# A hybrid decoder layer on one core: when ScalarE makes the decays of the state-space scans

## The chip, the core and the metric

The kernel runs on one core of a Trainium2 chip. Its time is the device time of one execution in microseconds (us). Before the change it took 2337.83 us, the median of three runs (2331.14, 2337.83 and 2346.82).

The engines have short names in the profile: PE is TensorE (PEld its weight loads), DVE is VectorE, ACT is ScalarE, POOL is GpSimd and SP is SyncE, which here only issues transfers.

## What is computed

One layer of a decoder for 2048 tokens of width 1024, with 16 learned meta tokens in front. A normalised input goes through one combined projection into two branches: a Mamba-2 state-space branch (SSD, 16 heads of 64 channels in 4 groups, state 128, chunks of 128 tokens) and a gated linear attention (GLA, 4 heads). Both outputs are gated by sigmoids, projected and added, and an output projection, a residual and a last norm follow. The change concerns the SSD branch:

```python
da = (dt * a).reshape(b, nc, chunk, h).transpose(0, 3, 1, 2)
da_cum = jnp.cumsum(da, axis=-1)
seg = da_cum[..., :, None] - da_cum[..., None, :]
decay = jnp.exp(jnp.where(causal, seg, -jnp.inf))
scores = jnp.einsum('bzthn,bzshn->bhzts', cc, bc)
y_diag = jnp.einsum('bhzts,bzsh,bzshp->bzthp', scores * decay, dtc, xc)
...
def step(s, inp):
    st, dec = inp
    return dec[..., None, None] * s + st, s
...
y_off = jnp.einsum('bzthn,bzhpn,bhzt->bzthp', cc, prev, jnp.exp(da_cum))
return (y_diag + y_off).reshape(b, l, h, p), final
```

The "decays" are `decay` of one chunk for the four heads of one group: a tile of 128 x 4 x 128, which is then multiplied by the masked scores.

## The kernel before

**Two phases.** The first phase (about 0 to 1500 us) runs the projections and both branches for four blocks of 512 tokens. The second phase merges the branches and projects the result out. The change is in the first.

**Projections and scans side by side.** For each block the program goes through four SSD groups (`ssd_proj`) and then four GLA heads (`gla_proj`). Each projection is a generator that yields after every piece of some 24 to 48 wide matmuls. After each piece one `step()` runs every scan that has begun, up to its own next `yield`. So the scan of group g is written in between the projection pieces of group g + 1. For a group there are six pieces: two of `proj_tok`, then four of `proj_feat`, one for each of x0, x1, B and C.

**Emptying the banks.** A projection accumulates in PSUM banks called `pj`, of which there are three. A feature piece takes one bank, in block 0 two, because of the meta tokens. ScalarE empties it with a copy into `cin` (L472) and a scaled copy into `acc` (L473); VectorE adds the three other taps of the convolution (L477), ScalarE takes a Tanh (L480), VectorE finishes the SiLU (L481). The gate chain of a block (`gates`) also uses `pj` banks and has an Abs (L435), an Exp (L437) and a Ln (L438) on ScalarE, and scans on VectorE.

**The SSD scan of one group.** `fetch_cb` (L490) issues, from ScalarE's queue, a transfer that spreads the cumulative decay of four heads and 128 tokens to all 128 partitions (tile `cb`, three buffers). The scan's pieces are then:

- the masked scores of all four chunks: four matmuls (L522) and one multiply by the triangle (L524, tile `scm`);
- `before(c)`: three transposes into a `pt` bank (L538), three VectorE multiplies out of it (L541 to L544), a ScalarE copy of B (L547), and the decay: four Relus with a per-partition bias (L550), one Exp (L552), and VectorE's multiply with the masked scores (L553), into a `sq` tile `dm` (five buffers, one of which holds `scm`);
- `after(c)`: four matmuls that read `dm` (L562), more matmuls with the state (L563, L565), the state update on GpSimd and VectorE (L567, L568), VectorE's output chain (L570 to L575), and on ScalarE a Square with an accumulator for the norm (L577);
- at the end the norm (L592), transposes (L597) and the stores.

**The order of work.** PE's and SyncE's instructions keep the order in which they are written. The order on ScalarE, VectorE and GpSimd is chosen at compile time by a scheduler that simulates the program's time; it may put an instruction ahead of others written earlier if its inputs are there. `tc.keep_in_program_order(ins)` adds one edge for the scheduler: `ins` comes behind the instruction that was written just before it on the same engine. It is an order of issue, not a wait for the end of that instruction.

Of the kernel before, what the change touches and what calls it, by code (L numbers as in the profile page):

```python
# [7 lines left out]
F32 = mybir.dt.float32  # L8
# [3 lines left out]
AF = mybir.ActivationFunctionType  # L12
ALU = mybir.AluOpType

P = 128
# [4 lines left out]
NCH = BLK // P  # L20
# [5 lines left out]
NSQ = 5  # L26
# [14 lines left out]
def trunk_kernel(ctx: ExitStack, tc: tile.TileContext, xm, xmt, w_feat, w_tok, w_zm, w_br, w_o,  # L41
                 cf32, cmsk, pvec, fnw, hvec, gw2, out):
    nc = tc.nc
# [5 lines left out]
    def mk(pool, shape, dt, tag, **kw):  # L49
        cnt[0] += 1  # L50
        return pool.tile(shape, dt, tag=tag, name=f"{tag}_{cnt[0]}", **kw)
# [66 lines left out]
    wk = first.enter_context(tc.tile_pool(name="wk", bufs=2))  # L118
# [6 lines left out]
    def bank(pool, tag):  # L125
        return mk(pool, [P, 512], F32, tag)
# [97 lines left out]
    def rstd_of(ssq, n, scale):  # L224
        r = mk(sm, [P, 4], F32, "rstd")
        nc.vector.tensor_scalar(r[:, :n], ssq, scale, EPS, op0=ALU.mult, op1=ALU.add)
        nc.gpsimd.tensor_tensor(r[:, :n], r[:, :n], mhalf[:, :n], op=ALU.pow)
        return r
# [114 lines left out]
    def new_block(b, u):  # L343
        o = Block()
        o.b, o.u = b, u
        o.m0 = META if b == 0 else 0
        o.tt = o.m0 + BLK
        o.segs_all = [(0, o.tt // 2), (o.tt // 2, o.tt // 2)] if b == 0 else [(0, BLK)]
        o.segs_real = [(o.m0, BLK)]
        o.starts = [o.m0 + c * P for c in range(NCH)]  # L350
        o.chunks = ([(0, META)] if o.m0 else []) + [(a, P) for a in o.starts]
        o.ci0 = 1 if o.m0 else 0
        o.nck = len(o.chunks)
        for nm in ("tkd", "tkc", "wde", "ecu", "dec"):
            setattr(o, nm, mk(bpool, [P, 5, NH], F32, nm, bufs=2))
        o.cumd = mk(dpool, [NH, BLK], F32, "cumd")
        o.g_all = mk(bpool, [P, GH, META + BLK], F32, "g_all")
        o.alr = mk(bpool, [P, 5, 48], F32, "alr")
        o.mov = lambda kt, a, n: tuple(t[:, kt, a:a + n] for t in u)
        return o  # L360
# [125 lines left out]
    cbs = {}  # L486

    def fetch_cb(o, g, c):
        cbs[g, c] = cb = mk(wk, [P, 4, P], F32, "cb", bufs=3)
        nc.scalar.dma_start(cb, o.cumd[4 * g:4 * g + 4, c * P:(c + 1) * P].unsqueeze(0).to_broadcast([P, 4, P]))  # L490

    def ssd_scan(o, g, feats, zs):
        m0, ci0 = o.m0, o.ci0
        tkd, tkc, wde, ecu, dec = o.tkd, o.tkc, o.wde, o.ecu, o.dec
        x0, x1, bf, cf = feats
        fetch_cb(o, g, 0)
        yield
        hs = slice(4 * g, 4 * g + 4)

        def hb(t, n):  # L500
            return t.unsqueeze(2).to_broadcast([n, 4, 64])

        if m0:
            ps = bank(pt, "pt")
            for j, f in enumerate((x0, x1, bf)):
                nc.tensor.transpose(ps[:META, j * P:(j + 1) * P], f[:, :META], ident)
            xw = mk(wk, [P, 4, 64], F32, "c1", bufs=NC1)
            nc.vector.tensor_tensor(xw[:META], ps[:META, :256].rearrange("p (a c) -> p a c", c=64),
                                    hb(wde[:META, 0, hs], META), op=ALU.mult)
            btm = mk(wk, [P, P], F32, "bt")  # L510
            nc.scalar.activation(btm[:META], ps[:META, 256:384], AF.Copy)

        def meta_state():
            ps = bank(pc, "pc")
            nc.tensor.matmul(ps[:, :256], btm[:META], xw[:META].rearrange("p a c -> p (a c)"),
                             start=True, stop=True)
            nc.vector.tensor_copy(s_ssd[:, g], ps[:, :256])

        sc = bank(pc, "pc")
        for c in range(NCH):  # L520
            a = m0 + c * P
            nc.tensor.matmul(sc[:, c * P:(c + 1) * P], bf[:, a:a + P], cf[:, a:a + P], start=True, stop=True)  # L522
        scm = mk(wk, [P, NCH, P], F32, "sq", bufs=NSQ)
        nc.vector.tensor_tensor(scm, sc.rearrange("p (c t) -> p c t", t=P),  # L524
                                tri.unsqueeze(1).to_broadcast([P, NCH, P]), op=ALU.mult)
        yt = mk(wk, [P, NCH, 256], F32, "tok4", bufs=NT4)
        ssq = mk(sm, [P, 4], F32, "ssq")
        held = {}

        def before(c):  # L530
            a = m0 + c * P
            ci = ci0 + c
            if c + 1 < NCH:
                fetch_cb(o, g, c + 1)
            cb = cbs.pop((g, c))
            ps = bank(pt, "pt")
            for j, f in enumerate((x0, x1, bf)):
                nc.tensor.transpose(ps[:, j * P:(j + 1) * P], f[:, a:a + P], ident)  # L538
            px = ps[:, :256].rearrange("p (h c) -> p h c", c=64)
            xdt = mk(wk, [P, 4, 64], F32, "c1", bufs=NC1)  # L540
            nc.vector.tensor_tensor(xdt, px, hb(tkd[:, ci, hs], P), op=ALU.mult)  # L541
            xw = mk(wk, [P, 4, 64], F32, "c1", bufs=NC1)
            nc.vector.tensor_tensor(xw, px, hb(wde[:, ci, hs], P), op=ALU.mult)
            nc.vector.tensor_tensor(yt[:, c].rearrange("p (h c) -> p h c", c=64), px,  # L544
                                    hb(d_skip[:, hs], P), op=ALU.mult)
            bt = mk(wk, [P, P], F32, "bt")
            nc.scalar.activation(bt, ps[:, 256:384], AF.Copy)  # L547
            dm = mk(wk, [P, 4, P], F32, "sq", bufs=NSQ)
            for h in range(4):
                nc.scalar.activation(dm[:, h], cb[:, h], AF.Relu, scale=-1.0,  # L550
                                     bias=tkc[:, ci, 4 * g + h:4 * g + h + 1])
            nc.scalar.activation(dm, dm, AF.Exp, scale=-1.0)  # L552
            nc.vector.tensor_tensor(dm, dm, scm[:, c].unsqueeze(1).to_broadcast([P, 4, P]), op=ALU.mult)  # L553
            held[c] = xdt, xw, bt, dm

        def after(c):
            a = m0 + c * P
            ci = ci0 + c
            xdt, xw, bt, dm = held.pop(c)
            py = bank(pc, "pc")  # L560
            for h in range(4):
                nc.tensor.matmul(py[:, h * 64:(h + 1) * 64], dm[:, h], xdt[:, h], start=True, stop=True)  # L562
            nc.tensor.matmul(py[:, 256:512], cf[:, a:a + P], s_ssd[:, g], start=True, stop=True)  # L563
            pst = bank(pc, "pc")
            nc.tensor.matmul(pst[:, :256], bt, xw.rearrange("p a c -> p (a c)"), start=True, stop=True)  # L565
            sv = s_ssd[:, g].rearrange("p (h c) -> p h c", c=64)
            nc.gpsimd.tensor_tensor(sv, sv, hb(dec[:, ci, hs], P), op=ALU.mult)  # L567
            nc.vector.tensor_tensor(s_ssd[:, g], s_ssd[:, g], pst[:, :256], op=ALU.add)  # L568
            yo = mk(wk, [P, 4, 64], F32, "c1", bufs=NC1)
            nc.vector.tensor_tensor(yo, py[:, 256:512].rearrange("p (h c) -> p h c", c=64),  # L570
                                    hb(ecu[:, ci, hs], P), op=ALU.mult)
            yof = yo.rearrange("p a c -> p (a c)")
            nc.vector.tensor_tensor(yof, yof, py[:, 0:256], op=ALU.add)
            nc.vector.tensor_tensor(yof, yof, yt[:, c], op=ALU.add)
            nc.vector.tensor_tensor(yt[:, c], yof, zs[:, c], op=ALU.mult)  # L575
            jk = mk(wk, [P, 256], BF16, "junk", bufs=1)
            nc.scalar.activation(jk, yt[:, c], AF.Square, accum_out=ssq[:, c:c + 1])  # L577

        before(0)
        yield  # L580
        if m0:
            meta_state()
            yield
        for c in range(1, NCH):
            before(c)
            after(c - 1)
            yield
        after(NCH - 1)
        yield
        r = rstd_of(ssq, 4, 1.0 / 1024)  # L590
        for c in range(NCH):
            nc.scalar.activation(yt[:, c], yt[:, c], AF.Identity, scale=r[:, c:c + 1])  # L592
        yield
        for j in range(2):
            ps = bank(pt, "pt")
            for c in range(NCH):
                nc.tensor.transpose(ps[:, c * P:(c + 1) * P], yt[:, c, j * P:(j + 1) * P], ident)  # L597
            yo = mk(wk, [P, BLK], F32, "gg", bufs=4)
            nc.scalar.activation(yo, ps, AF.Identity, scale=hsw[:, 2 * g + j:2 * g + j + 1])
            nc.scalar.dma_start(y_left[0][o.b][2 * g + j], yo)  # L600
# [226 lines left out]
    with tc.manual_schedule(engines={mybir.EngineType.PE, mybir.EngineType.SP}):  # L827
        for b in range(nblk):
            o = new_block(b, next_u[b])
# [343 lines left out]
```

## Time and profile before

| | |
|---|---|
| median of three runs | 2337.83 us |
| the profiled execution | 2339.7 us |
| its span, first to last instruction | 2337.9 us |
| PE busy | 2247.7 us, 96% |
| PEld busy | 1959.0 us, 84% |
| VectorE busy | 1548.3 us, 66% |
| ScalarE busy | 1180.1 us, 50% |
| GpSimd busy | 673.3 us, 29% |
| mean granted clock of TensorE | 0.985 |
| data moved by DMA | 518.05 MB |

A group in the profile is named by line, engine, operation and tiles, with its count and mean time. A row of the timeline gives the start in us, the duration in us, engine, line, operation, output and input tiles, and how many equal instructions are merged; in brackets stands how long the engine was idle before it and what ended that. A row of waits gives the engine, tile and line that waited, the engine and line waited for, the total in us, how often, and the longest. Matmuls overlap in the pipeline, so their durations are longer than the distance between their starts. PE's clock is given as the share of full speed that was granted.

### The profile page before, as it was taken

What the parts mean: (1) busy time and instruction counts of PE and PEld (TensorE: products, weight loads), DVE (VectorE), ACT (ScalarE), POOL (GpSimd) and SP (SyncE); (2) the same over time, 40 slices, a digit from 0 to 9 for tenths busy, and PEclk for the clock granted to TensorE, in tenths of its full rate; (3) what the DMA queues carried; (4) which work ended last, traced back from release to release, by engine and by line L of the source; (5) the groups of instructions that cost most, each with busy time, mean ns of one, the idle gap of its engine ahead of it and who ended that gap; (6) DMA issues with size and microseconds to landing.
All of it is one profiled execution on the core that took longest, in us unless ns stands there. A gap on an engine that the chain in (4) does not pass through costs nothing. (4 is left out here: it accounts for less than half of the span.)

```text
span 2337.9 us, 36478 instructions
## 1 busy us (share of the span) xinstructions
PE 2247.7 (96%) x12641; PEld 1959.0 (84%) x12641; DVE 1548.3 (66%) x2895; ACT 1180.1 (50%) x2758; POOL 673.3 (29%) x681
## 2 busy tenths in 40 slices
PE   7999999999999999999999999889999999999998
PEld 7899988888878989888988898768888778778786
DVE  5676766676675666576567555764578855678866
ACT  5666644465544455544455534454554445554543
POOL 4344433122221122211112100207424254313231
PEclk9999999999999999999999999889999999999999
DMA  8666866767785666786676655357577876777753
GB/s 304 226 203 213 293 227 204 222 191 240 246 274 184 209 222 210 258 260 221 199 226 212 212 161 163 128 180 245 187 244 268 290 231 202 242 267 262 246 171 120
DMA packets 301545, 518.05 MB, mean 222 GB/s; under 512 B 27696, under 2 KB 143664, under 8 KB 301360
## 3 DMA queue, kind: packets, MB, share of 16 engines
q1 hardware_dynamic: 200400, 402.84, 53.4%
q10 hardware_dynamic: 100960, 112.88, 13.9%
q8 instruction: 99, 1.62, 0.3%
q14 instruction: 86, 0.70, 0.1%
HBM read 368.42 MB, written 147.19 MB: 221 GB/s over the span
## 5 line engine op out<-in xcount | busy, mean ns | idle before, releaser
L183 PE MATMUL pj<-u,whl 128*128 128x512 f32 (+1 forms) x1184 | 449.4, 380 | 15.5 <-ACT acc L473 6.0
L185 PE MATMUL pj<-u,whl 128*128 128x512 f32 (+1 forms) x1184 | 433.5, 366 | 1.4 <-POOL whl L164 0.8
L184 PE MATMUL pj<-u,whl 128*128 128x512 f32 (+1 forms) x1184 | 432.8, 366 | 0.0
L183 PE MATMUL pj<-whl,u 128*128 128x256 f32 (+1 forms) x992 | 289.3, 292 | 1.6 <-ACT u L296 1.5
L185 PE MATMUL pj<-whl,u 128*128 128x256 f32 (+1 forms) x992 | 282.6, 285 | 1.5 <-DVE u L298 1.4
L184 PE MATMUL pj<-whl,u 128*128 128x256 f32 (+1 forms) x992 | 282.3, 285 | 0.3 <-POOL whl L164 0.3
L183 PEld LDWEIGHTS pj<-u,whl 128*128 128x128 f32 x1184 | 227.1, 192 | 54.8 <-ACT acc L473 7.0
L183 PE MATMUL psa<-b,a 128*128 128x512 f32 x640 | 249.7, 394 | 15.0 <-ACT sn L931 11.3
L185 PEld LDWEIGHTS pj<-u,whl 128*128 128x128 f32 x1184 | 226.8, 192 | 37.8 <-POOL whl L164 1.9
L184 PEld LDWEIGHTS pj<-u,whl 128*128 128x128 f32 x1184 | 227.4, 192 | 33.4
L185 PE MATMUL psa<-b,a 128*128 128x512 f32 x640 | 250.8, 392 | 1.4 <-DVE a L915 1.4
L184 PE MATMUL psa<-b,a 128*128 128x512 f32 x640 | 250.2, 391 | 0.0
L894 DVE TENSOR_TENSOR b<-br,b 128x512 fp32r<-128x512 f32 x196 | 151.4, 794 | 62.7 <-ACT b L893 59.8
L183 PEld LDWEIGHTS pj<-whl,u 128*128 128x128 f32 x992 | 190.0, 192 | 3.0 <-ACT u L296 1.8
L185 PEld LDWEIGHTS pj<-whl,u 128*128 128x128 f32 x992 | 189.8, 191 | 2.2 <-DVE u L298 2.2
L184 PEld LDWEIGHTS pj<-whl,u 128*128 128x128 f32 x992 | 190.1, 192 | 1.0 <-POOL whl L164 0.6
L164 POOL TENSOR_TENSOR whl<-wr,whl 128x512 fp32r<-128x512 f32 (+1 forms) x100 | 135.7, 1365 | 186.7 <-ACT whl L163 145.6
L80 POOL TENSOR_TENSOR wr<-wr 128x256 f32<-128x256 f32 x80 | 66.0, 825 | 426.7 <-DMA wr<-y 173.7
L905 POOL TENSOR_TENSOR as<-ar,ar 128x512 f32<-128x512 f32 x40 | 56.3, 1407 | 455.6 <-DMA ar<-in_w_br 211.9
L893 ACT ACTIVATE b<-br 128x512 fp32r<-128x512 f32 x196 | 119.0, 627 | 118.7 <-DMA br<-br_t 46.0
L915 DVE TENSOR_TENSOR a<-ar,a 128x512 fp32r<-128x512 f32 x160 | 128.0, 816 | 72.2 <-ACT a L914 71.8
L477 DVE SCALAR_TENSOR_TENSOR acc<-cin,hcw,acc 128x512 f32<-128x512 f32 (+1 forms) x192 | 154.6, 805 | 30.5 <-ACT acc L473 29.3
(271 smaller groups left out, 5058.4 us busy)
## 6 DMA issues: line engine op xcount, KB each, us to landing
whl<-k_s SPq DMA_DIRECT2D x96, 512.0 KB, 4.4
whl<-k_g SPq DMA_DIRECT2D x96, 512.0 KB, 4.2
whl<-k_v SPq DMA_DIRECT2D x48, 512.0 KB, 3.8
whl<-k_z SPq DMA_DIRECT2D x36, 512.0 KB, 3.8
wr<-in_w_feat SPq DMA_DIRECT2D x64, 256.0 KB, 4.4
k_s<-whl SPq DMA_DIRECT2D x32, 512.0 KB, 3.7
cb<-cumd ACTq DMA_DIRECT2D x64, 256.0 KB, 5.8
y<-gg ACTq DMA_DIRECT2D x64, 256.0 KB, 4.5
```

The costliest lines, as they stand in the source:

```text
L80: nc.gpsimd.tensor_tensor(o, x, y, op=ALU.subtract)
L164: nc.gpsimd.tensor_tensor(hl[:, 1], raw, hl[:, 0].bitcast(F32), op=ALU.subtract)
L183: nc.tensor.matmul(ps, sh, mh, start=first, stop=False, **kw)
L184: nc.tensor.matmul(ps, sh, ml, start=False, stop=False, **kw)
L185: nc.tensor.matmul(ps, sl, mh, start=False, stop=last, **kw)
L477: nc.vector.scalar_tensor_tensor(acc, cin[:, k:k + tt], hcw[:, ti, k:k + 1], acc, op0=ALU.mult, op1=ALU.add)
L893: nc.scalar.activation(t[:, 0], raw, AF.Copy)
L894: nc.vector.tensor_tensor(t[:, 1], raw, t[:, 0].bitcast(F32), op=ALU.subtract)
L905: nc.gpsimd.tensor_tensor(s1, a21, a22, op=ALU.add)
L915: nc.vector.tensor_tensor(t[:, 1], src, t[:, 0].bitcast(F32), op=ALU.subtract)
```

## The change

The decay moves out of `before(c)` into a function of its own, `decay(c)`. It is written one piece earlier: `decay(0)` ahead of `before(0)`, `decay(1)` behind it, and in the loop `decay(c + 1)` behind `after(c - 1)`. Each of its four Relus and its Exp is kept in program order on ScalarE. The broadcasts of chunks 0 and 1 are issued in the scan's first piece, and those of chunks 2 and 3 behind `decay(0)` and `decay(1)`. The numbers of buffers do not change.

```diff
         fetch_cb(o, g, 0)
+        fetch_cb(o, g, 1)
         yield
...
-        held = {}
+        held, dms = {}, {}
+
+
+        def decay(c):
+            ci = ci0 + c
+            cb = cbs.pop((g, c))
+            dm = dms[c] = mk(wk, [P, 4, P], F32, "sq", bufs=NSQ)
+            for h in range(4):
+                tc.keep_in_program_order(
+                    nc.scalar.activation(dm[:, h], cb[:, h], AF.Relu, scale=-1.0,
+                                         bias=tkc[:, ci, 4 * g + h:4 * g + h + 1]))
+            tc.keep_in_program_order(nc.scalar.activation(dm, dm, AF.Exp, scale=-1.0))
+            nc.vector.tensor_tensor(dm, dm, scm[:, c].unsqueeze(1).to_broadcast([P, 4, P]), op=ALU.mult)
+            if c + 2 < NCH:
+                fetch_cb(o, g, c + 2)
 
         def before(c):
             a = m0 + c * P
             ci = ci0 + c
-            if c + 1 < NCH:
-                fetch_cb(o, g, c + 1)
-            cb = cbs.pop((g, c))
...
-            dm = mk(wk, [P, 4, P], F32, "sq", bufs=NSQ)
-            for h in range(4):
-                nc.scalar.activation(dm[:, h], cb[:, h], AF.Relu, scale=-1.0,
-                                     bias=tkc[:, ci, 4 * g + h:4 * g + h + 1])
-            nc.scalar.activation(dm, dm, AF.Exp, scale=-1.0)
-            nc.vector.tensor_tensor(dm, dm, scm[:, c].unsqueeze(1).to_broadcast([P, 4, P]), op=ALU.mult)
-            held[c] = xdt, xw, bt, dm
+            held[c] = xdt, xw, bt
 
         def after(c):
...
-            xdt, xw, bt, dm = held.pop(c)
+            xdt, xw, bt = held.pop(c)
+            dm = dms.pop(c)
...
+        decay(0)
         before(0)
+        decay(1)
         yield
...
             before(c)
             after(c - 1)
+            if c + 1 < NCH:
+                decay(c + 1)
             yield
```

## The prediction

> **What bounds the kernel now.** I read the busy shares first, then a table by stage, then who waits for whom, then the order of time around the waits.
>
> ```profile
> PE 2247.7 (96%) x12641; PEld 1959.0 (84%) x12641; DVE 1548.3 (66%) x2895; ACT 1180.1 (50%) x2758; POOL 673.3 (29%) x681
> ```
>
> TensorE (PE) is busy for 2247.7 us of 2337.9, so all its idle time is 90 us. The change touches only the state-space scans, so I cut out their four stretches, one per block of 512 tokens (columns: stretch, its length, PE, PEld, DVE, ACT and POOL busy, granted clock, DMA share, GB/s).
>
> ```profile
> 50.00:300.00 250.00, 236.47 (x1750) 224.14 (x1749) 175.19 (x320) 157.91 (x402) 108.40 (x99) 0.97 0.70 235
> 480.00:660.00 180.00, 177.94 (x1032) 155.55 (x1031) 124.47 (x266) 102.63 (x263) 48.72 (x69) 0.99 0.74 235
> 844.00:1024.00 180.00, 176.82 (x1027) 154.67 (x1026) 124.12 (x267) 102.35 (x260) 47.22 (x69) 0.99 0.73 232
> 1207.00:1380.00 173.00, 172.85 (x1015) 151.83 (x1015) 118.03 (x253) 97.30 (x246) 35.31 (x53) 1.00 0.65 203
> ```
>
> PE idles 13.5 us in block 0 (250 - 236.47), then 2.1, 3.2 and 0.2 us. That is 19 us in all: whatever the decays cost today, no more than this and some lost clock can come back. PE's order is written out by hand and does not change, so a PE wait that goes is won nearly whole, and one that comes is lost nearly whole. The waits of PE, of the first stretch and (last line) of the decays' readers in the whole run:
>
> ```profile
> PE pj L183 <- ACT acc L473: 6.0, 4, 4.2
> PE pj L183 <- ACT g_all L435: 4.4, 2, 3.1
> ...
> PE pc L562 <- DVE sq L553: 1.7, 1, 1.7
> ```
>
> PE waited for a decay itself (L562 reads what L553 wrote) once, 1.7 us. The larger waits are for a PSUM bank of the projections that ScalarE (ACT) had not yet emptied (L473, L435). ScalarE in order of time before the 4.2 us wait, and PE's first matmul after it:
>
> ```profile
> 138.66 1.56 ACT L550 ACTIVATE sq<-cb,tkc 128x128 f32<-128x128 f32 x5
> ...
> 141.29 0.97 ACT L550 ACTIVATE sq<-cb,tkc 128x128 f32<-128x128 f32 x3
> 142.17 0.61 ACT L552 ACTIVATE sq<-sq 128x512 f32<-128x512 f32 x1
> ...
> 143.37 1.13 ACT L552 ACTIVATE sq<-sq 128x512 f32<-128x512 f32 x2
> 145.22 1.28 ACT L550 ACTIVATE sq<-cb,tkc 128x128 f32<-128x128 f32 x4 [0.72 <-DMA cb<-cumd]
> 146.40 0.37 ACT L472 ACTIVATE cin<-pj 128x264 f32<-128x264 f32 x1
> ...
> 147.28 0.59 PE L183 MATMUL pj<-u,whl 128*128 128x264 f32 x1 [4.19 <-ACT acc L473]
> ```
>
> This is the finding that matters. Nothing holds the decays back today, so the scheduler has put all four chunks of the group at the front of ScalarE's order: 16 Relus (in four rows of 5, 4, 3 and 4; the second is left out) and three of the four Exps run from 138.66 to 146.40, the last four Relus behind a broadcast that had not landed (0.72). Only then come the copies (L472, and L473 behind it) that free PE's bank.
>
> **What the change does, part by part.** No instruction is added or removed: 256 Relus, 64 Exps, 64 multiplies, 64 broadcasts as before. It changes when they come.
>
> *The burst becomes shorter.* At a group's first working piece only chunks 0 and 1 are written; chunk 2 comes one piece on, chunk 3 another. By the rows above a decay is four Relus, 1.28 us, and an Exp, 0.57 (1.13 for two), so 1.8 us, and two are 3.7. In the 4.19 us wait the copy L472 could then start near 143.1 (138.66, two decays, and the 0.7 us of other work that lay between the first Exp and the next two), not at 146.40: 3.3 us won. The other waits on L473, 6.0 - 4.2 = 1.8 us, were partly of this kind: I take 0.7 (bounds 0 and 1.8). The 3.1 us wait for L435 began the same way:
>
> ```profile
> 78.70 1.55 ACT L550 ACTIVATE sq<-cb,tkc 128x128 f32<-128x128 f32 x5
> ...
> 82.88 0.46 ACT L435 ACTIVATE g_all<-pj,pv 128x264 f32<-128x264 f32 x1
> ```
>
> Here 12 Relus and an Exp stood ahead, 4.2 us. Two decays of 1.8 us would stand ahead at worst (0.5 won), one at best (2.4 won); I take 1.5. Together 5.5 us, bounds 3.8 and 7.5.
>
> *Clock lost behind those waits.* The granted clock is column eight here.
>
> ```profile
> 84.00:88.00 4.00, 4.00 (x23) 4.00 (x22) 1.27 (x2) 4.00 (x10) 0.00 (x0) 0.57 0.98 319
> ...
> 147.00:151.00 4.00, 3.72 (x17) 3.72 (x18) 2.93 (x3) 3.15 (x7) 1.48 (x2) 0.50 1.05 372
> ```
>
> In the 4 us after the first wait 0.43 of the clock was missing (1.7 us), after the second 0.50 (2.0 us). I count the second, whose wait nearly goes, and not the first, which is only shortened: 2.0 us, bounds 0 and 3.7.
>
> [...]
>
> *Chunk 0's decay.* Its Exp now follows its own four Relus and need not stand behind those of chunks 1 and 2 (eight Relus, 2.5 us). Today chunk 0 is just in time:
>
> ```profile
> 576.03 0.69 DVE L553 TENSOR_TENSOR sq<-sq,sq 128x512 f32<-128x512 f32 x1 [3.06 <-ACT sq L552]
> ...
> 577.24 0.45 PE L562 MATMUL pc<-c,sq 128*128 128x64 f32 x3
> ...
> 584.82 0.45 PE L562 MATMUL pc<-c,sq 128*128 128x64 f32 x3
> ```
>
> It ends 0.5 us before its reader (the third row is chunk 1's, one piece or 7.6 us on). So the 1.7 us at L562 should go; I take all of it (bounds 0 and 1.7).
>
> *Broadcasts two chunks ahead.* ScalarE issues the same 64 transfers of 256 KB, in the median 5.8 us from issue to landing:
>
> ```profile
> cb<-cumd ACTq DMA_DIRECT2D x64, 256.0 KB, 5.8
> ```
>
> Two are now issued a piece before the first decay, and the third and fourth behind decays 0 and 1, a piece or more before their use. A piece of 7.6 us covers the landing, so I count nothing. If the cover were gone, Relus would wait as in the row at 145.22, 0.7 us a time. Nothing moves on SyncE's queue or GpSimd's.
>
> *What the hold adds.* The first Relu of chunk c + 1 is held behind the last ScalarE instruction written before it, which is the Square (L577) of chunk c - 1. That Square waits for VectorE's whole output chain. So chunks 2 and 3, ready today long before use, get a new wait, and what stands behind them in ScalarE's order (L472 and L473 of the next piece, the Tanh) waits too; behind L472 and L473 stands PE. Time left from the Square of chunk c - 1 to PE's use of chunk c + 1, first, tightest and last of 32 such pairs:
>
> ```profile
> 107.02 0.40 ACT L577 ACTIVATE junk<-tok 128x256 bf16<-128x256 f32 x1
> 118.63 0.45 PE L562 MATMUL pc<-c,sq 128*128 128x64 f32 x3
> ...
> 872.60 0.42 ACT L577 ACTIVATE junk<-tok 128x256 bf16<-128x256 f32 x1 [1.59 <-DVE tok L575]
> 875.88 1.00 PE L562 MATMUL pc<-c,sq 128*128 128x64 f32 x8
> ...
> 1361.07 0.42 ACT L577 ACTIVATE junk<-tok 128x256 bf16<-128x256 f32 x1 [0.53 <-DVE tok L575]
> 1370.38 1.00 PE L562 MATMUL pc<-c,sq 128*128 128x64 f32 x8
> ```
>
> These leave 11.6, 3.3 and 9.3 us. The mean of the 32 is 8.1; three are 3.3 (chunk 3 of group 0 in blocks 1 to 3, where the gate chain also loads VectorE), the next is 5.8. What must fit in: Square and its accumulator read 0.5, decay 1.8, multiply 0.7, so T = 3.0 us with nothing in between, and more by what VectorE and ScalarE have queued. Summing what T exceeds over the 32 pairs gives nothing at 3.0, 5 us at T = 5, 14.5 at 7, 44 at 9. I take T = 5, two queued instructions on each engine: 5 us lost, bounds 0 and 14.5.
>
> *Copies of block 0.* There a piece takes two of three PSUM banks, so a decay of 1.8 us just ahead of L472 is felt at once. It concerns eight decays. Nothing is the lower bound; the upper is that half of each shows, 7.2 us. I take 1.5, near the lower end, since the Square falls in the middle of a piece there as in the pair at 107.02.
>
> **The sum.** Won: 5.5 + 2.0 + 1.7 = 9.2 us. Lost: 5 + 1.5 = 6.5. Net 2.7 us won. The profiled execution took 2339.7 us (span 2337.9), 1.9 above the median 2337.83; carried to the median the forecast is 2335.1 us. Ends: most won (7.5 + 3.7 + 1.7) and nothing lost, 12.9 won (2325); least won (3.8), most lost (21.7), 18 lost (2356).
>
> **Rivals.** *The hold starves PE.* One mechanism: ScalarE reaches the held Relus late, because the Square stands behind VectorE, and in 32 places PE waits for the decay. For: VectorE fills 70% of these stretches, and the Square's own row shows it waiting (1.59). Against: the mean gap is 8.1 us, far above 3.0. It decides from T = 8 us on (26 us lost); at T = 9, 44 us lost and 9 won give 2373 us.
>
> *The burst was hidden anyway, or the hold does not hold.* The edge goes only to the one instruction before; and in blocks 1 to 3 PE hardly waited in these stretches. Against: the 4.19 us wait has the burst in front of it. It gives 2338 us, 3 either way.
>
> *All of the scans' idle time goes.* 19 us of PE idle, and the clock: 0.03 of 250 us and 0.01 of 360, 11 us. At most 30 us, 2308. Against: the two waits of the first stretch shown make up 10.4 of its 13.5 us, not all of that is the burst's, and the rest has other causes.
>
> **How the numbers follow.** Forecast 0.46, burst hidden 0.20, PE starved 0.24, all idle gone 0.10. The first two lie within 1% (23 us, about what a measurement of this kernel can tell from no change): same 0.66, slower 0.24, faster 0.10. The forecast's own range is 2325 to 2356. The range given, 2320 to 2364, goes a little into both outer cases and leaves out about 2 in 10.
>
> **What would show it.** Right: 10 or fewer Relus in a row at a group's start; the 4.2 us wait on L473 below 1.5; no wait of L562 on chunk 0; VectorE's idle time before L553 smaller. Half right: L562 waiting for chunk 3 in group 0 of blocks 1 to 3. Wrong: L562 waiting in most groups (the hold starves PE), or ScalarE still running 16 Relus ahead of L472, or PE's waits growing in a stage that the change does not touch.

## The result

The changed kernel takes 2345.5 us in the median (2340.4 to 2350.9), the kernel before 2335.9 in the same series: a ratio of 1.0043, 95% interval 1.0032 to 1.0054. The change costs 10 us (0.0043 x 2336). A gain of 2.7 us was forecast.

**The stretches.** The page's first row after, and the four stretches of the scans by the table by stage (columns as before):

```profile
PE 2252.4 (96%) x12641; PEld 1961.2 (84%) x12641; DVE 1546.3 (66%) x2895; ACT 1178.7 (50%) x2758; POOL 672.6 (29%) x681
50.00:300.00 250.00, 236.93 (x1723) 224.27 (x1721) 170.26 (x314) 155.69 (x400) 102.64 (x97) 0.96 0.68 232
480.00:660.00 180.00, 176.22 (x1038) 154.56 (x1037) 119.30 (x256) 101.53 (x258) 44.22 (x68) 0.98 0.71 225
844.00:1024.00 180.00, 174.94 (x1037) 153.67 (x1036) 118.35 (x254) 100.21 (x255) 45.68 (x67) 0.98 0.70 222
1207.00:1380.00 173.00, 171.95 (x1035) 151.69 (x1035) 114.98 (x249) 95.96 (x244) 31.24 (x51) 1.00 0.63 201
```

The other engines do the same work as before. PE's idle time has not shrunk in block 0 (13.1 us, before 13.5) and has grown in the other three (3.8, 5.1 and 1.0 us, before 2.1, 3.2 and 0.2), with a clock that is 0.01 lower in three of the four. The waits of PE over the whole run show new rows in place of the old ones:

```profile
PE pj L183 <- DMA whl<-k_g: 7.6, 2, 4.5
...
PE pj L183 <- ACT acc L473: 5.2, 3, 3.0
...
PE pc L569 <- DVE sq L541: 3.7, 3, 3.0
PE pj L183 <- ACT g_all L435: 3.1, 2, 2.1
```

The first is a wait for weights (`k_g`, the projection weights of the GLA heads), which the change does not touch. Before it was

```profile
PE pj L183 <- DMA whl<-k_g: 3.2, 2, 1.9
```

**Where the time is lost.** PE's order is fixed, so the same instruction can be looked up in both timelines; the difference of its starts is the lag at that place. One such pair, the transposes at the end of group 2 in block 2, before and after:

```profile
978.22 1.04 PE L597 MATMUL pt<-cst,tok 128*128 128x128 f32 x8
```

```profile
991.32 1.04 PE L608 MATMUL pt<-cst,tok 128*128 128x128 f32 x8
```

The lag there is 13.1 us. The same at other places, for the kernels of this study (us against the profiled execution of the kernel before; places by its times; the experiments are told below):

| place in the kernel before | 77.7 | 140.9 | 163.4 | 592.4 | 616.1 | 956.6 | 978.2 | 1026.2 | 1439.5 |
|---|---|---|---|---|---|---|---|---|---|
| after | 1.1 | 9.1 | 2.3 | 7.0 | 9.5 | 7.6 | 13.1 | 9.5 | 10.5 |
| e7_own_rows | 0.4 | 4.3 | -2.5 | -1.4 | -5.2 | -4.3 | -6.0 | -8.7 | -6.8 |
| e8_before_own_rows | -0.7 | -0.7 | -0.5 | 0.7 | -3.1 | -2.9 | -4.6 | -8.1 | -7.3 |
| e12_own_rows_late_groups | 0.1 | 0.2 | -5.7 | -6.6 | -10.4 | -12.2 | -13.9 | -17.4 | -17.2 |
| e14_late_groups | -0.8 | -2.3 | -8.1 | -6.1 | -4.6 | -4.9 | -1.4 | -5.0 | -3.7 |
| e16_groups_1_and_3 | 0.3 | 0.5 | -5.4 | -2.8 | -4.9 | -5.0 | -2.8 | -6.1 | -5.7 |
| e17_store_from_gpsimd | 0.7 | 4.7 | -2.1 | -0.5 | -2.2 | -2.0 | 3.8 | 0.3 | 1.7 |

After loses in group 0 of block 0 (to 140.9: 8.0 us), wins at the next group's start (6.8 us), and loses again just before 616.1 (2.5 us) and 978.2 (5.5 us). A further 4.7 us go in smaller steps between 163.4 and 592.4, where e7 loses 1.0; no experiment followed them up. A lag is that of one execution, and the kernel before stands here with one that took 3.8 us more than its median. Even kernels alike up to a place differ: at 140.9 after has 9.1 and e7 4.3, with every engine's order the same up to 200 us, because after lost clock behind a wait there (0.50 granted in the next 4 us) and e7 did not (1.00; the last section). At 1439.5 the first phase ends.

**The burst is gone, as forecast.** ScalarE after, at the start of group 1 in block 0, where 16 Relus stood before:

```profile
144.00 1.26 ACT L538 ACTIVATE sq<-cb,tkc 128x128 f32<-128x128 f32 x4
145.29 0.63 ACT L540 ACTIVATE sq<-sq 128x512 f32<-128x512 f32 x1
...
146.60 1.27 ACT L538 ACTIVATE sq<-cb,tkc 128x128 f32<-128x128 f32 x4
...
148.29 0.62 ACT L540 ACTIVATE sq<-sq 128x512 f32<-128x512 f32 x1
149.80 0.39 ACT L472 ACTIVATE cin<-pj 128x264 f32<-128x264 f32 x1 [0.89 <-PE pj L185]
```

Eight Relus and two Exps, and the copy L472 then waits for PE, no longer PE for it.

**Group 0 of block 0 pays for it.** Two new waits of PE, and what ScalarE and VectorE did ahead of them:

```profile
91.13 0.20 ACT L661 ACTIVATE gl<-g_all 128x1 f32<-128x1 f32 x1 [2.13 <-DVE g_all L443]
92.33 0.21 ACT L659 ACTIVATE gl<-g_all 128x4 f32<-128x4 f32 x1 [1.00 <-DVE g_all L443]
...
92.64 1.28 ACT L668 ACT_TABLE_LOAD   x1
...
94.05 0.37 ACT L472 ACTIVATE cin<-pj 128x264 f32<-128x264 f32 x1
94.93 0.59 PE L183 MATMUL pj<-u,whl 128*128 128x264 f32 x1 [2.97 <-ACT acc L473]
...
123.43 0.40 ACT L584 ACTIVATE junk<-tok 128x256 bf16<-128x256 f32 x1
...
127.07 0.63 ACT L540 ACTIVATE sq<-sq 128x512 f32<-128x512 f32 x1
...
130.23 1.75 DVE L541 TENSOR_TENSOR sq<-sq,sq 128x512 f32<-128x512 f32 x1
132.03 1.33 PE L569 MATMUL pc<-c,sq 128*128 128x64 f32 x5 [2.96 <-DVE sq L541]
```

At 91 us ScalarE stands in small gate copies (L661, L659) that wait for VectorE's scans, and a table load, ahead of the copy that frees PE's bank. At 123 us the Square (L584) of chunk 1 lets chunk 3's decay go; from its start to the end of the multiply are 8.5 us, since copies, gate instructions and scans lie in between. In this execution lost clock came behind each of the two waits as well (0.50 in the 4 us behind each), behind the second one not in e7 and e17 (the last section).

**The weights come late.** In blocks 1 and 2, SyncE issues the next block's row loads (L256) into `acc` tiles, of which there are two, and the weights `k_g` behind them. SyncE, and PE's first matmul with these weights, before:

```profile
964.60 3.88 SPq L256 DMA_DIRECT2D acc<-in_xm  x2
968.59 0.85 SPq L159 DMA_DIRECT2D whl<-k_g  x2
972.59 0.50 PE L183 MATMUL pj<-u,whl 128*128 128x512 f32 x1 [1.34 <-DMA whl<-k_g]
```

and after:

```profile
974.12 4.20 SPq L256 DMA_DIRECT2D acc<-in_xm  x2
978.72 0.80 SPq L159 DMA_DIRECT2D whl<-k_g  x2
983.35 0.79 PE L183 MATMUL pj<-u,whl 128*128 128x512 f32 x1 [4.47 <-DMA whl<-k_g]
```

PE had come to this place 7.6 us later than before (the lag at 956.6); the row loads and the weights came 9.5 and 10.1 us later. Their buffer is freed by the SiLU (L481), behind the Tanh (L480), of one of the last SSD projection pieces, which run beside the scan of group 2. ScalarE before, and ScalarE and VectorE after:

```profile
961.68 0.63 ACT L480 ACTIVATE act<-acc 128x512 f32<-128x512 f32 x1 [3.20 <-DVE acc L477]
963.18 0.52 ACTq L83 DMA_DIRECT2D br_t<-wr  x1
```

```profile
971.95 0.52 ACTq L83 DMA_DIRECT2D br_t<-wr  x1
972.52 0.63 ACT L480 ACTIVATE act<-acc 128x512 f32<-128x512 f32 x1 [5.37 <-POOL wr L80]
973.18 0.91 DVE L481 SCALAR_TENSOR_TENSOR act<-act,acc 128x512 f32<-128x512 f32 x1 [2.67 <-ACT act L480]
```

The scheduler's new order puts a store of the side unit (L83) ahead of that Tanh, and the store waits for GpSimd's subtractions (L80). Then follow, one behind the other, the SiLU at 973.18, the row loads at 974.12, the weights at 978.72 and PE at 983.35.

### The profile page after: what moved, and what is told of

Same layout as the page of the kernel before. It is cut to its first block, busy times and chain, and to the rows that moved or that the text cites. A ratio compares the mean times of both kernels' runs of the same rounds, so it can differ in the third digit from the quotient of the medians.

```text
span 2343.6 us, 36481 instructions
## 1 busy us (share of the span) xinstructions
PE 2252.4 (96%) x12641; PEld 1961.2 (84%) x12641; DVE 1546.3 (66%) x2895; ACT 1178.7 (50%) x2758; POOL 672.6 (29%) x681
## 3 DMA queue, kind: packets, MB, share of 16 engines
q10 hardware_dynamic: 100960, 112.88, 13.9%
## 5 line engine op out<-in xcount | busy, mean ns | idle before, releaser
L183 PE MATMUL psa<-b,a 128*128 128x512 f32 x640 | 249.6, 394 | 10.5 <-ACT sn L942 8.1
L164 POOL TENSOR_TENSOR whl<-wr,whl 128x512 fp32r<-128x512 f32 (+1 forms) x100 | 133.9, 1346 | 185.7 <-ACT whl L163 136.5
L80 POOL TENSOR_TENSOR wr<-wr 128x256 f32<-128x256 f32 x80 | 64.4, 805 | 423.3 <-DMA wr<-u 173.4
L477 DVE SCALAR_TENSOR_TENSOR acc<-cin,hcw,acc 128x512 f32<-128x512 f32 (+1 forms) x192 | 155.7, 811 | 40.6 <-ACT acc L473 39.4
```

The source lines that it names most:

```text
L80: nc.gpsimd.tensor_tensor(o, x, y, op=ALU.subtract)
L164: nc.gpsimd.tensor_tensor(hl[:, 1], raw, hl[:, 0].bitcast(F32), op=ALU.subtract)
L183: nc.tensor.matmul(ps, sh, mh, start=first, stop=False, **kw)
L477: nc.vector.scalar_tensor_tensor(acc, cin[:, k:k + tt], hcw[:, ti, k:k + 1], acc, op0=ALU.mult, op1=ALU.add)
```

## The experiments

All ratios are to the kernel before, run on the same chip in the same series (its medians 2333.1 to 2335.7 us). "After" beside a name means that the edit is made to the changed kernel. In edited kernels the line numbers of the profile move by a few: L563 in e2, L571 in e10 and L575 in e11 to e16 are the matmuls that read a decay (L562 before, L569 after).

**Which part costs?** First the hold alone, each way, the broadcasts alone, and the blocks apart.

e1_no_hold (after):

```diff
-                tc.keep_in_program_order(
-                    nc.scalar.activation(dm[:, h], cb[:, h], AF.Relu, ...))
-            tc.keep_in_program_order(nc.scalar.activation(dm, dm, AF.Exp, scale=-1.0))
+                nc.scalar.activation(dm[:, h], cb[:, h], AF.Relu, ...)
+            nc.scalar.activation(dm, dm, AF.Exp, scale=-1.0)
```

> The changed kernel without the hold: the decay is written in its new place and the broadcasts come two ahead, but the Relus and Exps are free. Theory A (the hold alone costs): ScalarE's compiled order is nearly that of before, with the burst of 16 Relus back, so the time is that of before, 0 us (within 3), and the 4.2 us wait on L473 in block 0 is back. Theory B (the broadcasts, now two ahead, delay the weight loads that PE waits for): +10 us as in the changed kernel, with the waits of PE on k_g weights at 3 to 4 us each.

2339.6 us, ratio 1.0022 (1.0006 to 1.0039). Without the hold ScalarE's order is that of the kernel before but for 10 of 2758 instructions, and the burst is back (L473 4.2 us). So the hold makes the change; moving the decay's lines alone does next to nothing to the order. That this is still 5 us over the kernel before is not explained: its profiled execution was 2331.1 us.

e2_hold_only (the kernel before):

```diff
-                nc.scalar.activation(dm[:, h], cb[:, h], AF.Relu, ...)
-            nc.scalar.activation(dm, dm, AF.Exp, scale=-1.0)
+                tc.keep_in_program_order(
+                    nc.scalar.activation(dm[:, h], cb[:, h], AF.Relu, ...))
+            tc.keep_in_program_order(nc.scalar.activation(dm, dm, AF.Exp, scale=-1.0))
```

> The kernel before with the hold alone: the decays stay written in before(c), the broadcasts one ahead, the Relus and Exps are kept in program order. Theory A: the burst is gone as in the changed kernel, and a chunk's decay comes one piece later than there, so the time is +10 us or more (up to +25) and PE waits for decays (L562) in several groups. Theory B: the broadcasts are as before, so 0 us (within 3).

2356.6 us, ratio 1.0094 (1.0075 to 1.0112), 22 us slower. Held at the old place, the decays are late for PE itself:

```profile
PE pc L563 <- DVE sq L554: 8.6, 5, 2.4
```

The piece by which the change moves them ahead is what brings this wait down to the 3.7 us of L569 after.

e3_broadcasts_only (the kernel before):

```diff
         fetch_cb(o, g, 0)
+        fetch_cb(o, g, 1)
...
-            if c + 1 < NCH:
-                fetch_cb(o, g, c + 1)
...
+            if c + 2 < NCH:
+                fetch_cb(o, g, c + 2)
```

> The kernel before with the broadcasts written two chunks ahead and nothing else. The compiled order of every engine is that of before, so 0 us under every theory; what it shows beside 0 is what this measurement can tell.

2333.2 us, ratio 0.9999 (0.9985 to 1.0012). The orders of ScalarE, VectorE and GpSimd are those of the kernel before, instruction for instruction. The broadcasts ahead cost and bring nothing by themselves.

e5_block0_only and e6_blocks123_only (the whole change, in these blocks alone):

```diff
+        new = bool(o.m0)        # e6: not o.m0
```

> The whole change in block 0 only, blocks 1 to 3 as before. The trace of the changed kernel has lost 6.5 us by the end of block 0 and 10.5 by the end of the first phase. Theory A: +3 to +7 us, with PE's waits of 3 us on L473 and of 3 us for chunk 3's decay in group 0, and without the 4.2 us wait of before. Theory B: the long waits on weights lie in blocks 1 and 2, so 0 us (within 3).

> The whole change in blocks 1 to 3 only, block 0 as before. Theory A: +2 to +6 us, from small waits spread over the groups. Theory B: +10 us, from the waits on k_g weights near 610 and 980 us, which were 1.9 and 1.3 us before and 3.2 and 4.5 after.

2334.3 us, ratio 1.0009 (0.9995 to 1.0023), and 2343.1, ratio 1.0038 (1.0025 to 1.0051). In block 0 gain and loss cancel. The loss is in blocks 1 to 3, and there PE waits 7.8 us for `k_g` in e6, against 1.4 us for decays.

**Is it SyncE's queue?** The row loads get tiles of their own, so that no transfer ahead of the weights can be late for the scans' sake. e7_own_rows is after with this edit, e8_before_own_rows the kernel before with it:

```diff
-                    xt = mk(wk, [P, META + BLK], F32, "acc")[:, :BLK]
+                    xt = mk(wk, [P, BLK], F32, ("kdt", "atp")[i], bufs=2)
```

> The changed kernel, but the rows of the next block's input that SyncE loads at the first GLA head (L256) go to two tiles that stand idle there (kdt, atp) and not to the two acc tiles of the convolution. Theory C (the hold makes VectorE's and ScalarE's chain of group 3 late; the row load on SyncE's queue waits for an acc tile, and the weights behind it, k_g, come late): PE's waits on k_g near 615 and 980 us fall from 3.2 and 4.5 us to below 1, and the time comes within 3 us of the kernel before, or below it. Theory A (the loss is spread: PE waits for decays and copies in many groups): it stays 8 to 10 us slower than before.

> The kernel before with the rows in idle tiles as in e7_own_rows. Its own waits on k_g were 1.9 and 1.3 us, so 2 to 4 us faster than before. Against it e7_own_rows shows what the hold costs without SyncE's queue: theory C 0 to 3 us, theory A 8 to 10.

e7: 2329.6 us, ratio 0.9981 (0.9972 to 0.9990); e8: 2327.6, ratio 0.9977 (0.9964 to 0.9989). SyncE's rows in e7, to be held against 974.12 and 978.72 above:

```profile
955.96 0.38 SPq L256 DMA_DIRECT2D atp<-in_xm  x1
957.01 3.05 SPq L159 DMA_DIRECT2D whl<-k_g  x2
```

No wait for `k_g` is left in either. The Tanh of e7 still stands behind the store (L83 at 961.31, the SiLU at 962.54), but the weights have gone out at 957.01. Near 616 and 978 the edit moves little beside the work on the rows themselves in the engines' orders; near 200 to 260 us it moves more. It is worth 14.5 us to the changed kernel (1.0043 - 0.9981) and 5.4 to the kernel before: about 9 of the 10 us lost, give or take 4 by the intervals, were on this queue. With it out of the way the change itself comes to +0.0004, 1 us. In the table e7 wins at 616.1 and 978.2 what after loses there (from 2.5 lost to 3.8 won, and from 5.5 lost to 1.7 won: 13.5 of the 14.5 us).

**An attempt to take the hold forward.** e9_hold_ahead_of_square (after) and e13_own_rows_hold_ahead_of_square (e7):

```diff
             before(c)
-            after(c - 1)
             if c + 1 < NCH:
                 decay(c + 1)
+            after(c - 1)
```

> The changed kernel with decay(c + 1) written ahead of after(c - 1), so that its first Relu is held behind the copy of B (L559) of chunk c and not behind the Square of chunk c - 1. In the compiled order the Tanh of the third feature piece (L480) is ahead of the side unit's store (L83) again, as before. Theory C: the k_g waits go back to 1 to 2 us and the time to within 3 us of before, or below, since the 4.2 us burst wait stays away. Theory A (any hold late in the group costs): +8 to +10 us as in the changed kernel.

> Rows with tiles of their own, and the decay of chunk c + 1 written ahead of the output chain of chunk c - 1 instead of behind it, so that the held Relus follow the Square of chunk c - 2. Both cures together. If each takes away its own part (e7_own_rows: 14.7 us below the changed kernel; e9_hold_ahead_of_square: 7.5 below), and the second's part was mostly the same queue, this is 0 to 3 us below e7_own_rows, 2326 to 2330; if the second's part was the lateness of the decays themselves, 5 to 8 below it, 2321 to 2325.

e9: 2338.1 us, ratio 1.0013 (1.0000 to 1.0027), 7 us below the changed kernel, with `k_g` waits of 1.1 and 1.5 us. e13: 2330.7, ratio 0.9990 (0.9977 to 1.0003), 2 us above e7, neither of the figures expected. So e9's gain came from the queue; with the rows apart, decays written ahead of the Square do not help.

**Which decays make the rows late, and by what?** e10_store_held (after) and e17_store_from_gpsimd (after) ask whether it is the store:

```diff
-            store.dma_start(dst[j][:, :, cs], src)
+            ins = store.dma_start(dst[j][:, :, cs], src)
+            if tag == "wr":
+                tc.keep_in_program_order(ins)
```

```diff
-                yield from make_sums(wpool, "wr", NWR, *sums[key], j, c, nc.scalar)
+                yield from make_sums(wpool, "wr", NWR, *sums[key], j, c, nc.gpsimd)
```

> The changed kernel with one more hold: the DMA instruction on ScalarE that stores a side unit's row sums (L83) keeps its place in the program, so that the scheduler no longer puts it ahead of the Tanh pieces of the chunk (L480). In the changed kernel the Tanh waited 5.37 us behind it for GpSimd (972.52), the old rows' buffer was freed late, and the weights k_g behind the row loads on SyncE's queue came 3.2 and 4.5 us late. Theory C1 (the store that overtook the Tanh makes the rows late): the two k_g waits go back to 1 to 2 us, and the time is 4 to 10 us below the changed kernel, 2335 to 2341. Rival C2 (the held decays among the copies of piece 3 are enough to make them late): k_g waits stay above 3 us and the time stays within 3 us of the changed kernel, 8 to 10 us above the kernel before.

2488.2 us, ratio 1.066 (1.0636 to 1.0684): 154 us slower, expected by neither. The held stores come late, so the `wr` tiles are free late, and the side unit's own loads (L76) now stand at the head of SyncE's queue in front of the weights:

```profile
SPq L76 <- DMA br_t<-wr: 138.9, 12, 21.0
...
PE pj L185 <- DMA whl<-k_z: 46.8, 9, 10.3
PE pj L185 <- DMA whl<-k_g: 41.5, 6, 9.2
PE pj L185 <- DMA whl<-k_s: 28.2, 6, 5.3
```

It says nothing on the Tanh, but it is the mechanism of the loss again, some fifteen times as large.

> The changed kernel whole, but the side units' stores (L83) are issued by GpSimd behind its own subtractions, and not by ScalarE, so that no Tanh can stand behind a store that waits for GpSimd. If the store ahead of the Tanh makes the rows late: no wait of L480 on L80, k_g waits of 2 us or less, and 5 to 12 us below the changed kernel (2345.5), 2333 to 2341. If the held decays do it: k_g waits of 3 us or more, and within 3 us of the changed kernel.

2338.3 us, ratio 1.0024 (1.0006 to 1.0043), 4 to 5 us below the changed kernel. The wait of block 1 falls from 3.17 to 1.87 us: there the store was it. That of block 2 stays, at 4.77 us. There the subtractions now run while VectorE adds the convolution taps ahead of the Tanh (GpSimd and VectorE in e17):

```profile
960.60 2.20 POOL L80 TENSOR_TENSOR wr<-wr,wr 128x256 f32<-128x256 f32 x2
...
962.14 0.94 DVE L581 TENSOR_TENSOR c<-c,tok 128x256 f32<-128x256 f32 x1
963.00 1.75 DVE L477 SCALAR_TENSOR_TENSOR acc<-cin,hcw,acc 128x512 f32<-128x512 f32 x1
963.38 0.81 POOL L80 TENSOR_TENSOR wr<-wr 128x256 f32<-128x256 f32 x1
```

In e17 an L477 of this shape takes 0.74 us in the median, an L581 0.42. So the store is half an answer, with other lateness ready to take its place.

e14_late_groups, e15_groups_1_and_2 and e16_groups_1_and_3 are the change in some groups of every block, the rest as in the kernel before:

```diff
+        new = g > 0             # e15: g in (1, 2); e16: g in (1, 3)
...
-        decay(0)
+        if new:
+            decay(0)
```

> The change in groups 1 to 3 of every block; group 0 as in the kernel before, and the rows' buffers as they were. Theory D1 (the last group's decays among the copies make the rows' buffer late): the k_g waits stay at 3 us or more each, as in the changed kernel, and the time is 6 to 12 us above e12_own_rows_late_groups (2318.8), 2325 to 2331. Rival D2 (the lateness came from group 0, through the order that follows from it): k_g waits of 1 to 2 us as in the kernel before, and the time 5 us above e12 at most (what own rows bring the kernel before), 2319 to 2324.

> The change in groups 1 and 2 of every block alone, rows' buffers as they were. D1: the k_g waits are those of the kernel before (1.9 and 1.3 us) or less, the gain of block 0 (the 4.2 us wait and the clock, 6 to 7 us) is kept, and the time is 6 to 9 us below the kernel before, 2325 to 2328, and not above e14_late_groups. D2: the same time as e14_late_groups within 2 us.

> The change in groups 1 and 3 of every block, rows' buffers as they were; group 2, at whose end the next rows are asked for, is as in the kernel before. If what stands in group 2 alone makes the rows late, the k_g waits are 1 to 2 us as in the kernel before, and with the gain of block 0 the time is 5 to 9 us below the kernel before, 2326 to 2331. If any change in the block's order does it, the k_g waits are 3 us or more and the time is within 2 us of e14_late_groups and e15_groups_1_and_2, 2333 to 2336.

2334.2, 2334.7 and 2329.2 us; ratios 0.9995 (0.9983 to 1.0008), 0.9997 (0.9985 to 1.0009) and 0.9987 (0.9970 to 1.0005). The waits for `k_g` in e14, e15 and e16:

```profile
PE pj L183 <- DMA whl<-k_g: 7.1, 2, 3.6
```

```profile
PE pj L183 <- DMA whl<-k_g: 6.4, 2, 3.4
```

```profile
PE pj L183 <- DMA whl<-k_g: 3.3, 2, 1.9
```

The last group, suspected in the first two expectations, is not it: e15 leaves it alone and the waits stay. Group 2 is: with its decays as before, the waits are those of the kernel before (3.2 us). That fits where the rows are asked for, at the end of this group's scan (just ahead of 978.2 in the table). e14's ratio is 0.0060, 14 us, above that of e12 (below), more than the 6 to 12 of its first theory.

**A version that beats both.** Rows with their own tiles, and the change without group 0: in block 0 alone (e11_own_rows_block0_late_groups, `new = o.m0 and g > 0`) or in all blocks (e12_own_rows_late_groups, `new = g > 0`).

> The next block's row loads have tiles of their own (as in e7_own_rows), and the change is made only in block 0 and there only in groups 1 to 3; the rest is the kernel before. If the burst ahead of L472 in groups 1 to 3 of block 0 is worth what the traces said (the 4.2 us wait and the clock behind it, 6.8 us) and the new waits of the change come from its group 0 and from blocks 1 to 3, this is 6 to 8 us below e8_before_own_rows: 2320 to 2323, with no PE wait of 3 us on L569 in block 0. If the waits of block 0 only move to other places (as in e5_block0_only, 0.1% from the kernel before), it is within 2 us of e8_before_own_rows, 2326 to 2330.

> Rows with tiles of their own, and the change in groups 1 to 3 of every block. Against e11_own_rows_block0_late_groups it adds the change in blocks 1 to 3. If the change costs blocks 1 to 3 nothing once SyncE's queue is not blocked, it is within 2 us of that run; if the held decays themselves cost PE waits there (at most 3.7 us were seen on L569), 3 to 6 us above it.

e11: 2322.0 us, ratio 0.9953 (0.9937 to 0.9968). e12: 2318.8, ratio 0.9935 (0.9918 to 0.9952), 15 us below the kernel before and 25 below the changed one. The rows alone bring 5.4 (e8), groups 1 to 3 bring 9.8 more, and group 0, back in e7, takes 10.7 away. e11 is 5.6 us below e8, close to its first expectation (6 to 8). In e12 blocks 1 to 3 add 3 to 4 us more of gain, which neither theory had; the two intervals overlap, so this gain is not certain. In e12 PE waits 1.8 us in all for L473, and 0.9 for a decay:

```profile
PE pj L183 <- ACT acc L473: 1.8, 3, 0.9
...
PE pc L575 <- DVE sq L543: 0.9, 1, 0.9
```

## Why the prediction was wrong

**The burst (5.5 us won) and the clock behind it (2.0): right.** From 140.9 to 163.4 five kernels with the change in group 1 but not in group 0 win 5.8 to 5.9 us each (e11, e12, e14, e15, e16), and after 6.8. The step had 3.3 us of the L473 wait and 2.0 of clock for this place: the clock was 0.50 from 147.00 to 151.00 before and is 1.00 from 150.00 to 154.00 after. The wait for L435 fell from 3.1 to 2.1 us, a gain of 1.0 where 1.5 was taken. The clock behind it did not come back in after, as the sum had it: 0.57 in the next 4 us (before, 0.57 from 84.00). In e17 no clock was lost behind the same wait (2.13 us, at 83.06): PE's matmuls behind it start 0.12 us apart, in after 0.22.

**Chunk 0's wait (1.7 us won): right in size, not shown in cause.** The wait stood in front of group 3 in block 2; from 978.2 to 1026.2 the lag falls by 3.6 us, the wait (1.67 us) and as much clock again (0.57 in the 4 us behind it before, 1.7 us; 1.00 from 996 to 1010 after). But e8, with the old decays and other tiles for the rows, wins 3.5 there too, so that the new order of the Relus did it is not shown, and the clock behind the wait, which the step left out, may be chance.

**Broadcasts (nothing): right,** by e3. The seven waits of a Relu for its broadcast, 5.1 us of ScalarE's time before, are gone after. That no one had waited for them is not shown: the 0.72 us at 145.22 lie inside the 4.19 us wait of PE. e3 does not settle it, since a wait of 0.64 us stays in that place.

**The hold (5 us lost at T = 5): right in blocks 1 to 3, wrong in block 0.** e12 against e7 in the table's source gives group 0's price where the queue plays no part: about 1.3, 1.5 and 2.9 us in blocks 1, 2 and 3, 5.7 together, at chunk 3, which was named as the half-right case. But T is no one number: in group 0 of block 0 it was 8.5 us (123.43 to 131.98), with six copies and gate instructions on ScalarE between Relus and Exp, and the scans on VectorE in between. The pair at 107.02 with its 11.6 us of room seemed safe there; the pair behind it had 9.3 us before (Square at 116.76, use at 126.07), enough even for 8.5. But in the new order its Square stands behind the gate chain's Ln (L438) and two table loads, not ahead of them, and comes 6.7 us later, at 123.43, while PE was only 2.8 us later than before. The step took the Square's place from the old order.

**Copies of block 0 (1.5 us lost): too small.** The wait of 2.97 us at 94.93 and the clock of 0.50 in the 4 us behind it (2.0) are 5 us. The bound of 7.2 held, but by luck: what stood ahead of L472 was no decay but gate copies and a table load that the new order let in. Together with the wait at 132.03 group 0 of block 0 cost about 4 us on balance in e7 and 8 in after, which lost more clock.

**"Nothing moves on SyncE's queue or GpSimd's": the step that failed.** SyncE's transfers do keep their order (GpSimd's do not quite: some 50 of its 681 instructions stand elsewhere), but their time moved: the row loads wait for a buffer whose last reader sits behind the held decays and the store. 3.2 us of waiting for `k_g` became 7.6, with the clock behind it (0.50 in the 4 us behind each of the two waits, before 0.62 and 1.00), and e7 and e8 put 9 us on it (give or take 4). The cue was in the trace of before: PE already waited 1.9 and 1.3 us for `k_g`, behind row loads that waited for VectorE (L481; four waits of the row loads for it, 24.5 us in all). A wait that is already there, at the end of a chain through the engine that is reordered, has no slack left: what the chain comes later than PE, PE waits. In block 2 PE came 7.6 us later and the weights 10.1, which then took 4.63 us and not 4.00 from issue to PE's start, and the wait grew from 1.34 to 4.47 us. The working named the Tanh among what waits behind the held decays, but followed only the copies on to PE, and never asked who waits for the SiLU that follows the Tanh. Without this queue the change cost 1 us (e7 against e8), where 2.7 were to be won. "PE's waits growing in a stage that the change does not touch" stood on the list of what would show it wrong, without a price.

**The rivals.** "The hold starves PE" did not happen: L569 waited 3.7 us in three places, and 6.4 in five in e7. It happens when the decays are held without being moved ahead (e2). "The burst was hidden anyway" is refuted by the 5.8 us, "the hold does not hold" by e1. "All of the scans' idle time goes" (2308 us) was far off; the nearest is e12 with 2318.8, a different kernel.

**What stays open.** Which instruction in group 2 makes the SiLU late in block 2 (the store, the multiply between the taps, or the slow L477 beside GpSimd's L80 seen in e17) was not separated. Nor are the 5 us of e1 explained.

## What to carry over

Before an instruction is held or moved on one engine, list the buffers that the instructions behind it free, and look for a transfer at the head of an in-order queue that waits for one of them: everything behind that transfer is late too, weights included (here the rows by 9.5 us and the weights by 10.1), and a wait of 1 to 2 us that is already there says that no slack is left (here 1.9 and 1.3 us became 3.2 and 4.5). Price a hold by the fullest stretch in which it acts, not by the mean: here, with tiles of their own for the rows, the same edit won 10 us in three groups and lost 11 in the one beside the gate chain. And when a good change comes out slow, look for the one place that eats it, since two small edits around it (other tiles for the rows, group 0 left out) turned 10 us lost into 15 won.

## What the hardware showed beyond that

**The clock does not go by the length of a wait alone.** Rows of 4 us behind waits of PE: after, behind 2.12, 2.97, 2.96 and 4.47 us; then e16, behind 1.35 and 1.94 us (granted clock in column eight):

```profile
83.52:87.52 4.00, 4.00 (x20) 4.00 (x21) 0.94 (x2) 3.97 (x7) 0.00 (x0) 0.57 0.79 283
94.93:98.93 4.00, 4.00 (x18) 4.00 (x19) 3.11 (x3) 1.40 (x5) 1.53 (x2) 0.50 0.11 45
132.03:136.03 4.00, 4.00 (x14) 3.64 (x15) 4.00 (x7) 1.14 (x4) 1.68 (x2) 0.50 0.95 332
983.35:987.35 4.00, 4.00 (x9) 3.14 (x10) 0.00 (x0) 2.70 (x7) 0.26 (x1) 0.50 0.84 296
```

```profile
605.63:609.63 4.00, 4.00 (x18) 3.31 (x19) 0.21 (x2) 2.61 (x7) 1.01 (x1) 1.00 0.88 273
968.20:972.20 4.00, 4.00 (x11) 3.15 (x12) 0.50 (x2) 2.89 (x8) 1.20 (x2) 0.57 0.88 299
```

A wait of 1.35 us cost no clock here, 1.94 us cost 0.43 of 4 us, 2.97 us half. But the same wait at L569 that is followed by a clock of 0.50 in after (2.96 us, at 132.03) is followed by 1.00 in e7 (2.95 us, at 130.32) and in e17 (2.96 us, at 130.69): the eight matmuls that it held up took 1.97 us in after and 1.10 in e17. Between 50 and 1440 us of the kernel before and of after, 8 of PE's 18 waits of 1.25 to 3.2 us were followed by a lower clock (mean of the next 4 us, 0.50 to 0.64), and both longer ones (4.19 and 4.47 us, 0.50). In that stretch of these two profiles the clock is either full or half. The half lasts 3.41 us (before from 84.21, 111.52, 609.87, 702.02 and 988.74; after from 83.93 and 230.71) or 6.83 us (before from 145.65; after from 94.17, 131.72, 298.97, 616.41 and 981.64). Within each of the two profiles these starts lie whole multiples of 3.413 us apart: 8, 18, 154, 181 and 265 of them behind the first one before, 3, 14, 43, 63, 156 and 263 after. What decides whether such a stretch follows a wait is not shown. At L569 it made 3.1 us of difference: over this wait the lag of after grows by 6.3 us (from 2.8 to 9.1) and that of e7 by 3.2 (from 1.1 to 4.3).

**VectorE beside GpSimd.** The multiply L541 took 1.75 us at 130.23 in after, where its median is 0.69, while GpSimd subtracted weights (two L164 from 130.06, 3.04 us). L477 took 1.75 us at 963.00 in e17, where its median is 0.74, beside an L80 (0.81 us from 963.38). In after, 13 of the 64 L541 took more than 0.7 us (0.88 to 1.75), each with an L164 or an L80 of GpSimd running beside it. The other 51 took 0.67 to 0.69 us, five of them although an L80 ran for a part of their time. What makes them longer is not shown.
